# A two-layer diffusion trunk on one core: scheduling priority for the softmax steps, stores and bias tables placed anew, and four small changes of order

## The chip, the cores and the metric

One core of one Trainium2 chip runs the whole kernel in one launch. The metric is the device time of that launch in microseconds. TensorE (PE) does the matrix products and the transposes; VectorE (DVE), ScalarE (ACT) and GpSimd (POOL) do the elementwise work; SyncE (SP) issues most of the DMAs.

## The reference

The input is 1024 latent tokens and 256 context tokens of width 1024; there are two layers. Each layer is, per token group:

```python
h = rms_norm(x, norm_g) * (1 + scale) + shift          # shift, scale, gate from the conditioning
(aq, ak, av, ag, bq, bk, bv, bg, cx, cg, ga, gb, gc) = split(h @ w_in)
ya = window_attention(rope(norm(aq)), rope(norm(ak)), av, cached context k/v, sink) * silu(ag)
yb = neighbourhood_attention(rope(norm(bq)), ..., relative bias) * silu(bg)
yc = (linear_scan forward + backward of a gated recurrence on conv(cx)) * silu(cg)
z = sigmoid(ga) * (ya @ w_br[0]) + sigmoid(gb) * (yb @ w_br[1]) + sigmoid(gc) * (yc @ w_br[2])
x = x + gate * (z @ w_out)
```

Attention has 8 heads of 64 in each of two branches (A: a window of 128 tokens either side and a per-head sink; B: an 8 x 16 neighbourhood on the grid with a bias table). Latent queries read their local keys and 512 cached context keys in one softmax. All is float32; the kernel splits each operand in a high and a low part and does three products (or two) where it needs the precision.

## The kernel before, in words

Tokens lie along the free axis in three chunks: 0 and 1 are the latent halves of 512 tokens, 2 is the 256 context tokens. Activations have the 1024 features on 8 tiles of 128 partitions (`k`).

**Who sets the order.** PE's instructions run in the order in which the program emits them. A planner, `Weave`, sets that order: it has a clock of its own (`W.now`, in ns of estimated PE time), chains of dependent steps (the attention heads, the recurrence), and two queues of *dense* jobs (blocks of 24 matmuls of the input projection, `need` and `spare`) which it places where a chain is not yet due. `W.later(delay, fn)` runs `fn` when the clock has moved on by `delay`; `W.settle()` runs everything that is still waiting. The table `T` holds the delays. The dense blocks that stand between the steps of a chain are called filler below; they are finite in number. The other engines' order, and SP's, is made by a scheduler out of the whole program; `tc.high_priority(n)` lets what is emitted under it go ahead of other ready work that stands up to `n` places earlier, and `tc.keep_in_program_order` pins an instruction.

**Start (from `trunk`, `with pool("start")`).** The three chunks of x are loaded, transposed, normalised (`norm_apply`: on ACT `hhl`/`hhc`, on DVE `nt` and `hll`/`hlc`, for chunk 1 and chunk 2) while PE does gate blocks `gt`. `keep` stores the transposed x to DRAM (`x_d`), `constants` computes small per-layer columns, `bias_tables` builds B's bias tables through DRAM (`rp_d`, `t_d`, `bias_d`) with `W.later`. A gate block loads its weight (`wgt_r`, SP), casts it to the high part (`wgt_h`, ACT), subtracts for the low part (`wgt_l`, POOL), multiplies, and its result is copied (`tgt`, ACT) and stored (`g_d`, SP).

**Recurrence (`lru`).** Per feature block `f`, a conv on DVE (`xc`, split into `xh`, `xl`), then the gate products `lg`; `tiles["at", f]` is the planned time from which `lg` may be emitted.

**Attention (`attention`, `Group`).** Each branch has four pairs of heads (p = 0 to 3; B first, then A), each pair five groups of 256 queries (t0 = 0, 2, 8, 4, 6 in 128s; 8 is the context) with four score steps each. `score` (line 956) does: `sc`, the scores against the 512 cached keys (PE, one PSUM bank); DVE's minimum of `sc` (L976); `sl`, the local scores (PE, another bank); DVE's masked minimum (L992); for A the sink (L995 DVE, L996 ACT); ACT's two exponentials (L998 for `sc`, L1000 for `sl`). The banks `s` are two, so that the next `sc` has to wait for the exponential that frees its bank. `to_keys` transposes the exponentials (`pt`, three banks `t`) and splits them (`PT`, ACT L426 and DVE L427); `values` multiplies with V (`o`); `finish` adds and scales the result (Y: L1059 ACT, L1060 and L1066 DVE; `rt` is a transpose into a bank `t`). Beside it DVE and ACT normalise and rotate the next queries (`q_raw`, `q_sq`, `q_me`, L736 to L757).

**Merge and output.** `merge_jobs` makes `z`, `output_jobs` multiplies with `w_out` (blocks `po`, for chunks 0 and 2 together, then chunk 1), adds x, and in layer 0 takes the next layer's norm (`token_rstd`, whose product is `nps`, then `norm_apply`). A `tall` job goes through its features k once, for all of its chunks at each k; otherwise it finishes one chunk before the next.

## Time and profile before

| | |
|---|---|
| median of 3 runs | 3197.76 us (3196.37 to 3200.18) |
| the profiled execution | 3200.29 us, of which its span is 3198.5 us |
| PE busy | 3093.8 us (97%) |
| DVE busy | 1796.5 us (56%) |
| ACT busy | 1707.7 us (53%) |
| POOL busy | 974.9 us (30%) |
| granted PE clock, mean | 0.985 |
| moved by DMA | 435.03 MB, mean 136 GB/s |

PE is the engine that sets the time: the others are busy for little more than half of the span. As PE runs in the order of the program, any wait of one of its instructions holds up all that follow. A list of PE's waits gives, for each kind of waiting instruction, what released it, the total, how often and the longest; a timeline shows single instructions with the idle time before them and the releaser in square brackets. A table by windows gives PE's busy time and its granted clock (1.00 is full, 2.4 GHz; 0.50 is half, 1.2 GHz): busy time at half clock holds half the work.

### The profile page before, as it was taken

To read this page: it belongs to the slowest core of one execution; us is meant where nothing else is said; L and a number is where in the kernel's file an instruction comes from. 1 tells how busy PE (TensorE), PEld (TensorE's weight loads), DVE (VectorE), ACT (ScalarE), POOL (GpSimd) and SP (SyncE) were. 2 spreads that over 40 slices of the span, in tenths; PEclk is the share of its full clock that TensorE was granted. 3 is DMA by queue.
4 is the path that set the end of the run, shared out by engine and by line. 5 is a ranking of instruction groups with operands and counts; after the bars stand their busy time and mean duration, and the time that the engine had idled before them with its cause. 6 is when DMAs were issued, how large, how long until landed. Compare 5 with 4: busy or idle time off the path is not lost.

```text
span 3198.5 us, 48113 instructions
## 1 busy us (share of the span) xinstructions
PE 3093.8 (97%) x17421; PEld 2642.1 (83%) x17421; DVE 1796.5 (56%) x3293; ACT 1707.7 (53%) x3591; POOL 974.9 (30%) x815
## 2 busy tenths in 40 slices
PE   7899999999999999999999999999999999999999
PEld 5677788888888888888888778888888888888887
DVE  5565366666666664355464554665675666555531
ACT  5577355555555655443346864565555555544422
POOL 3554322223222121246343443221241222102632
PEclk9999999999999999999999999999999999999999
DMA  8554645535533232663442236545554333237543
GB/s 281 153 178 134 175 127 152 146 107 164 163 98 93 75 99 73 227 201 119 143 143 71 80 98 175 128 124 152 142 139 129 105 98 87 80 130 239 165 150 102
DMA packets 447434, 435.03 MB, mean 136 GB/s; under 512 B 75120, under 2 KB 368604, under 8 KB 445916
## 3 DMA queue, kind: packets, MB, share of 16 engines
q1 hardware_dynamic: 441212, 414.92, 43.6%
q0 software_dynamic: 5664, 16.83, 1.6%
q8 instruction: 137, 2.24, 0.3%
q14 instruction: 101, 0.83, 0.1%
q10 hardware_dynamic: 320, 0.21, 0.0%
HBM read 298.12 MB, written 137.29 MB: 136 GB/s over the span
## 4 chain that ended last, share of the span: by engine, by line
PE 78%; DVE 9%; ACT 4%; DMA 3%; issue 3%; POOL 2%; SPq 0%; ACTq 0%; DVEq 0%; POOLq 0%
PE gt L217 15%; PE sg L217 10%; PE br L217 7%; PE po L217 7%; PE o L217 6%; PE pt L224 6%; PE q L217 6%; PE k L217 4%; PE v L217 4%; PE sc L217 4%; PE sl L217 3%; PE cx L217 3%; PE lg L217 2%; DVE lR L686 1%; POOL acc L1236 1%
## 5 line engine op out<-in xcount | busy, mean ns | idle before, releaser
L426 ACT CAST PT<-pt 128x512 fp32r<-128x512 f32 (+2 forms) x528 | 272.5, 535 | 344.2 <-PE pt L224 340.0
L427 DVE TENSOR_TENSOR PT<-pt,PT 128x512 fp32r<-128x512 f32 (+2 forms) x528 | 321.9, 622 | 104.8 <-ACT PT L426 102.2
L976 DVE TENSOR_REDUCE st<-sc 128x1 f32<-128x512 f32 x256 | 176.6, 690 | 314.6 <-PE sc L217 314.2
L217 PE MATMUL gt<-hhl,wgt_h 128*128 128x512 f32 x736 | 301.5, 410 | 3.3 <-ACT wgt_h L421 3.3
L217 PE MATMUL gt<-hhl,wgt_l 128*128 128x512 f32 x736 | 292.5, 397 | 7.9 <-POOL wgt_l L422 7.9
L217 PE MATMUL gt<-hll,wgt_h 128*128 128x512 f32 x736 | 292.1, 397 | 0.0
L224 PE MATMUL pt<-cst,P 128*128 128x128 f32 x1856 | 271.8, 273 | 6.2 <-DVE Y L1066 3.8
L422 POOL TENSOR_TENSOR wgt_l<-wgt_r,wgt_h 128x512 fp32r<-128x512 f32 x110 | 176.6, 1613 | 324.4 <-ACT wgt_h L421 281.1
L224 PEld LDWEIGHTS pt<-cst,P 128*128 128x128 f32 x1856 | 217.2, 141 | 16.6 <-issue 7.8
L217 PE MATMUL po<-z,wpo_h 128*128 128x512 f32 (+1 forms) x768 | 212.9, 365 | 6.1 <-ACT z L426 4.9
L998 ACT ACTIVATE P<-sc,st 128x512 f32<-128x512 f32 x256 | 175.2, 684 | 57.9 <-DVE st L992 57.7
L217 PE MATMUL br<-yl,wbr_h 128*128 128x512 f32 (+1 forms) x576 | 205.1, 356 | 0.9 <-DVE yl L427 0.9
L217 PE MATMUL br<-yh,wbr_h 128*128 128x512 f32 (+1 forms) x576 | 204.7, 355 | 0.0
L217 PE MATMUL br<-yh,wbr_l 128*128 128x512 f32 (+1 forms) x576 | 204.4, 355 | 0.0
L217 PE MATMUL sc<-Kpast,Q 128*128 128x512 f32 x512 | 168.5, 410 | 28.6 <-ACT P L998 28.6
L422 POOL TENSOR_TENSOR wsg_l<-wsg_r,wsg_h 128x512 fp32r<-128x512 f32 x48 | 65.0, 1360 | 411.5 <-ACT wsg_h L421 289.2
L1000 ACT ACTIVATE P<-sl,st 128x384 f32<-128x384 f32 (+1 forms) x320 | 170.9, 534 | 16.0 <-DVE st L988 15.7
L217 PE MATMUL o<-PT,Vpast 128*128 128x256 f32 x1024 | 175.6, 292 | 3.6 <-DVE Y L1060 2.1
L217 PEld LDWEIGHTS gt<-hhl,wgt_l 128*128 128x128 f32 x736 | 139.9, 190 | 41.7 <-POOL wgt_l L422 9.2
L217 PEld LDWEIGHTS gt<-hhl,wgt_h 128*128 128x128 f32 x736 | 140.5, 191 | 34.8 <-issue 4.7
L217 PEld LDWEIGHTS po<-z,wpo_h 128*128 128x128 f32 x768 | 138.7, 194 | 29.5 <-ACT z L426 5.7
L217 PEld LDWEIGHTS gt<-hll,wgt_h 128*128 128x128 f32 x736 | 140.3, 191 | 25.5 <-issue 0.5
(350 smaller groups left out, 8562.7 us busy)
## 6 DMA issues: line engine op xcount, KB each, us to landing
Q<-q_d SPq DMA_DIRECT2D x160, 256.0 KB
gl<-g_d SPq DMA_DIRECT2D x48, 640.0 KB
wgt_r<-in_w_in_dram SPq DMA_DIRECT2D x110, 256.0 KB
g_d<-tgt SPq DMA_DIRECT2D x92, 256.0 KB
wa<-in_w_ada_dram POOLq DMA_DIRECT2D x64, 256.0 KB, 4.3
wpo_r<-in_w_out_dram SPq DMA_DIRECT2D x64, 256.0 KB
yg<-y_d SPq DMA_DIRECT2D x24, 640.0 KB
yr<-s_d SPq DMA_DIRECT2D x24, 640.0 KB
```

What stands on the lines that cost most here:

```text
L217: nc.tensor.matmul(out, a, b, start=start, stop=stop)
L224: nc.tensor.transpose(out, x, idn)
L422: nc.gpsimd.tensor_sub(lo, r, f32(hi))
L426: nc.scalar.copy(hi, x)
L427: nc.vector.tensor_sub(lo, x, f32(hi))
L686: nc.vector.tensor_tensor_scan(h, a, u, st if c0 < NLAT else 0.0, ALU.mult, ALU.add)
L976: nc.vector.tensor_reduce(cm, psc, AX.X, ALU.min)
L998: nc.scalar.activation(pt[:, nl * P:(nl + 4) * P], psc, AF.Exp, bias=m, scale=-1.0, accum_out=sums[:, t, x, 1:2])
L1000: nc.scalar.activation(pt[:, :nl * P], loc, AF.Exp, bias=m, scale=-1.0, accum_out=sums[:, t, x, 0:1])
L1236: (nc.vector if b == 0 and k >= KD - 2 else nc.gpsimd).tensor_add(z, z, g)
```

## The change

Seven edits:

- `score` runs under a priority of 400 (`AHEAD`), and so does the split of the transposed exponentials in `to_keys`.
- In layer 1, the gate products of the recurrence are planned 2500 ns later (`cv`), and the transposes of the cached keys (`kct`) 10000 ns behind their load where they were 7000 behind it.
- In layer 0's output, the norm's product for chunk 2 takes a bank `s` where it took the one bank `o`.
- The first block of `w_out` for chunks 0 and 2 is `tall`.
- At the start, the stores of x of chunks 1 and 2 come after both `norm_apply` and one by one, each behind one planned filler step; `constants` stands between the two chunks.
- Layer 1's rows of the bias tables are planned at 400000 + 20000 r ns where they were at 200000 + 3000 r.

```diff
--- before.py
+++ after.py
@@ -72,11 +72,12 @@
 
 
 EXP_LN = 6
+AHEAD = 400
 BEHIND = 2
 PSB = {"d": 2, "s": 2, "t": 3, "o": 1}
 LGB = ("s", "t")
 LDB = ("d", "t")
-T = dict(f1=9, f2=2, kc=7000, c0=10000, cq=1, gx=3, nx=8000, yo=1500, yi=1000, aq=9000, ac=7000, ms=2000, v=3200, tok=8600, scale=1100, t0=3400, tb=2200, o=2200, soft=7600, pace=9400, lg=320, lr=8500, cv=16000, le=4200)
+T = dict(f1=9, f2=2, kc=10000, c0=10000, cq=1, gx=3, nx=8000, yo=1500, yi=1000, aq=9000, ac=7000, ms=2000, v=3200, tok=8600, scale=1100, t0=3400, tb=2200, o=2200, soft=7600, pace=9400, lg=320, lr=8500, cv=16000, le=4200)
 
 
 class Weave:
@@ -621,7 +622,7 @@
             split(xh, xl, xc)
             W.mark(("conv", l, f))
             tiles[f] = (gh, gl, xc, xh, xl)
-            tiles["at", f] = W.now + T["cv"]
+            tiles["at", f] = W.now + T["cv"] + (2500 if l else 0)
 
         yield W.when(("cx", l, 0))
         conv(0)
@@ -954,6 +955,10 @@
 
 
             def score(g, s, i):
+                with tc.high_priority(AHEAD):
+                    g.score_of(s, i)
+
+            def score_of(g, s, i):
                 br, p = g.br, g.p
                 if g.st is None:
                     g.st = ap.tile([P, 36], F32, tag="st", name=f"st{g.name}", bufs=3)
@@ -1024,7 +1029,8 @@
                         transpose(pt[:, n * P:(n + 1) * P], g.P[g.units[s][i]][:, j * P:(j + 1) * P], ident)
                         n += 1
                 pq = ap.tile([P, 2, 512], F32R, tag="PT", name=f"PT{g.name}_{s}_{bi}", bufs=3)
-                split(pq[:, 0, :n * P], pq[:, 1, :n * P], pt[:, :n * P])
+                with tc.high_priority(AHEAD):
+                    split(pq[:, 0, :n * P], pq[:, 1, :n * P], pt[:, :n * P])
                 return pq
 
             def values(g, s, bank, pq, first, last):
@@ -1290,14 +1296,15 @@
                 add_square(l + 1, ci, k, xt, acc[ci], nc.vector.tensor_add)
 
                 def finish():
-                    token_rstd(l + 1, ci, acc[ci])
+                    token_rstd(l + 1, ci, acc[ci], "s" if ci == 2 else "o")
                     norm_apply(l + 1, ci, xs[ci], acc[ci], H)
                     W.mark(("x free", l, ci))
                 if k == KD - 1:
                     W.later(T["nx"], finish)
             return run
         return [(W.when(*[("Z", l, j) for j in range(KD)], *([("x free", l, free)] if free is not None and k else [])),
-                 job(I["w_out"][l], k * P, cis, lambda c: cols_of(Z, c), evac(k), f"po{l}_{cis[0]}_{k}"))
+                 job(I["w_out"][l], k * P, cis, lambda c: cols_of(Z, c), evac(k), f"po{l}_{cis[0]}_{k}",
+                     tall=len(cis) > 1 and k == 0))
                 for k in range(KD)]
 
 
@@ -1342,9 +1349,9 @@
             xs.append(xt)
         return xs
 
-    def keep(ci, xs):
+    def keep(ci, xs, ks=range(KD)):
         c0, N = CHUNKS[ci]
-        for k in range(KD):
+        for k in ks:
             ordered(dma(x_d[0][k][:, c0:c0 + N], xs[k][:, :N]))
 
 
@@ -1370,7 +1377,7 @@
                 W.later(20000 + 3000 * (3 * c + d), lambda c=c, d=d: shift(c, d))
         for l in range(DEPTH):
             for r in range(ROWS):
-                W.later(100000 + 100000 * l + 3000 * r, lambda l=l, r=r: rows(l, r))
+                W.later(400000 + 20000 * r if l else 100000 + 3000 * r, lambda l=l, r=r: rows(l, r))
 
     def fill(n):
         for _ in range(n):
@@ -1452,13 +1459,15 @@
             fill(T["f2"])
             token_rstd(0, 2, acc[2], "t", False)
             norm_apply(0, 1, xs[1], acc[1], H)
-            keep(1, xs[1])
             norm_apply(0, 2, xs[2], acc[2], H)
-            fill(9)
+            for ci in (1, 2):
+                for k in range(KD):
+                    fill(1)
+                    keep(ci, xs[ci], (k,))
+                fill(1)
+                if ci == 1:
+                    constants(0)
             starting.clear()
-            keep(2, xs[2])
-            constants(0)
-            fill(9)
             bias_tables()
         W.spare.extend((always, j((1, 2))) for j in jobs[:8])
         for l in range(DEPTH):
```

Three places in the order of the instructions show what the diff alone does not. Numbers behind a name are buffer numbers; the layer is left out of the names; lines of the changed kernel are a few higher.

**SP at the start, where the weight of gate block 7 (`wgt_0_70`) is loaded.** Before, right behind the stores of x of chunk 1:

```order
L1348 DMA x_d_6_78<-xi_6_719 128x512
L1348 DMA x_d_7_79<-xi_7_726 128x512
L413 DMA wgt_0_70_r_1082<-in_w_in_dram 128x4x128
L413 DMA wgt_0_70_r_1088<-in_w_in_dram 128x4x128
L413 DMA wcx_0_r_1134<-in_w_in_dram 128x4x128
L413 DMA wcx_0_r_1140<-in_w_in_dram 128x4x128
```

Now:

```order
L1355 DMA x_d_6_78<-xi_6_719 128x512
L711 DMA g_d_0_5_117<-tgt_0_50_0_1035 128x512
L1355 DMA x_d_7_79<-xi_7_726 128x512
L414 DMA wgt_0_70_r_1074<-in_w_in_dram 128x4x128
L414 DMA wgt_0_70_r_1080<-in_w_in_dram 128x4x128
L1355 DMA x_d_0_72<-xi_0_795 128x256
```

The loads now stand behind `g_d_0_5`, the store of the result of gate block 5, which reads the ACT copy `tgt_0_50`.

**ACT at the same place.** Before, the casts of that weight stood between the passes of `norm_apply` on chunk 1:

```order
L565 ACTIVATE hhl_2_234<-nt_1_2_935,mod_222 128x512
L565 ACTIVATE hhl_3_236<-nt_1_3_939,mod_222 128x512
L421 CAST wgt_0_70_0_h<-wgt_0_70_r_1082 128x512
L421 CAST wgt_0_70_4_h<-wgt_0_70_r_1088 128x512
L565 ACTIVATE hhl_4_238<-nt_1_4_943,mod_222 128x512
L565 ACTIVATE hhl_5_240<-nt_1_5_947,mod_222 128x512
```

Now they stand behind the passes on chunk 2 and two copies:

```order
L566 ACTIVATE hhc_4_985<-nt_2_4_983,mod_222 128x256
L566 ACTIVATE hhc_5_991<-nt_2_5_989,mod_222 128x256
L566 ACTIVATE hhc_6_997<-nt_2_6_995,mod_222 128x256
L710 COPY tgt_0_50_0_1035<-gt_0_50_0_914 128x512
L710 COPY tgt_0_60_0_1119<-gt_0_60_0_1086 128x512
L566 ACTIVATE hhc_7_1003<-nt_2_7_1001,mod_222 128x256
L422 CAST wgt_0_70_0_h<-wgt_0_70_r_1074 128x512
L422 CAST wgt_0_70_4_h<-wgt_0_70_r_1080 128x512
```

The copy `tgt_0_50` comes behind seven of the eight passes on chunk 2, and the casts behind all eight.

**DVE in branch A, p = 0, layer 0, from the first add of `Y_0_2` to the sink minimum of the first score step of group 4** (`st_0_4`). Before:

```order
L753 SCALAR_TENSOR_TENSOR q_1_1_raw<-q_1_1_sq,q_1_1_raw 128x512
L1060 TENSOR_TENSOR Y_0_2_9523<-o_0_2_9342,Y_0_2_9523 64x256
L757 STREAM_SHUFFLE q_1_1_sq<-q_1_1_raw 128x512
L1060 TENSOR_TENSOR Y_0_2_9523<-o_0_2_9342,Y_0_2_9523 64x256
L742 TENSOR_SCALAR q_1_2_me<-q_1_2_ms 128x256
L976 TENSOR_REDUCE st_0_4_9546<-sc_0_4_0_9548 128x1
L1066 TENSOR_TENSOR Y_0_2_9523<-Y_0_2_9523,rt_0_2_9560 128x256
L750 TENSOR_TENSOR q_1_2_raw<-q_1_2_raw,q_1_2_sq 128x256
L992 ISA sl_0_4_0_9552,st_0_4_9546<-sl_0_4_0_9552,mask_0_8743,st_0_4_9546 128x384
L992 ISA st_0_4_9546 128x1
L752 TENSOR_TENSOR q_1_2_sq<-q_1_2_me,q_1_2_sq 128x256
L995 TENSOR_TENSOR st_0_4_9546<-st_0_4_9546,sink_288 128x1
```

Now:

```order
L1066 TENSOR_TENSOR Y_0_2_9523<-o_0_2_9345,Y_0_2_9523 64x256
L754 SCALAR_TENSOR_TENSOR q_1_1_raw<-q_1_1_sq,q_1_1_raw 128x512
L1066 TENSOR_TENSOR Y_0_2_9523<-o_0_2_9345,Y_0_2_9523 64x256
L981 TENSOR_REDUCE st_0_4_9554<-sc_0_4_0_9556 128x1
L758 STREAM_SHUFFLE q_1_1_sq<-q_1_1_raw 128x512
L997 ISA sl_0_4_0_9560,st_0_4_9554<-sl_0_4_0_9560,mask_0_8746,st_0_4_9554 128x384
L997 ISA st_0_4_9554 128x1
L428 TENSOR_TENSOR PT_0_8_0_0_9573<-pt_0_8_0_0_9568,PT_0_8_0_0_9573 128x512
L1000 TENSOR_TENSOR st_0_4_9554<-st_0_4_9554,sink_288 128x1
```

Four passes of the query norm and the scaling of Y by `rt` went behind the sink minimum, the split of `PT_0_8` came in front of it, and the first add of Y now precedes the long pass `q_1_1_raw`.

**PE in the last group of layer 1's attention, around `sc_3_6_1`.** Before:

```order
L217 MATMUL sg_0_00_1_28559<-hhl_0_15404,wsg_0_00_0_l 128x512
L217 MATMUL sg_0_00_1_28559<-hhl_1_15406,wsg_0_00_0_h 128x512
L217 MATMUL sg_0_00_1_28559<-hll_1_15407,wsg_0_00_0_h 128x512
L217 MATMUL sg_0_00_1_28559<-hhl_1_15406,wsg_0_00_0_l 128x512
L217 MATMUL sc_3_6_1_28567<-Kpast_0_24169,Q_3_6_28327 128x512 x2
L217 MATMUL sl_3_6_1_28571<-Klat_0_24171,Q_3_6_28327 128x384 x2
L217 MATMUL o_3_4_28579<-PT_3_4_0_0_28539,Vpast_0_24453 128x256 x4
```

Now:

```order
L225 MATMUL pt_3_4_0_1_28607<-cst,P_3_4_0_28432 128x128
L225 MATMUL pt_3_4_0_1_28607<-cst,P_3_4_1_28472 128x128
L218 MATMUL sc_3_6_1_28616<-Kpast_0_24268,Q_3_6_28417 128x512 x2
L218 MATMUL sl_3_6_1_28620<-Klat_0_24270,Q_3_6_28417 128x384 x2
L218 MATMUL o_3_4_28628<-PT_3_4_0_0_28604,Vpast_0_24552 128x256 x4
L225 MATMUL pt_3_4_0_2_28633<-cst,P_3_4_0_28432 128x128
```

The filler (`sg_0_00`) is gone from in front of this score step, as from all places behind `sc_3_4_3`: 72 matmuls of it stood there before, and stand earlier now.

## Rows read from the trace of the kernel before

**Rows 1.** PE's waits: who waited, for whom; us in total, times, longest

```profile
PE sc L217 <- ACT P L998: 28.6, 12, 3.7
PE gt L217 <- POOL wgt_l L422: 7.9, 3, 5.9
PE lg L217 <- DVE xl L427: 5.5, 3, 1.8
PE pt L224 <- DVE Y L1066: 3.8, 2, 1.9
PE nps L217 <- DVE nw L533: 2.1, 1, 2.1
PE cx L217 <- ACT tgt L709: 1.8, 1, 1.8
PE kct L224 <- DMA kc<-in_cache_kb_dram: 1.8, 1, 1.8
```

**Rows 2.** PE's timeline, layer 0, branch A, p = 0: start us, us, instruction, [idle before]

```profile
918.69 0.39 PE L217 MATMUL gt<-hll,wgt_h 128*128 128x512 f32 x1
918.92 0.39 PE L217 MATMUL gt<-hhl,wgt_l 128*128 128x512 f32 x1
922.92 1.22 PE L217 MATMUL sc<-Kpast,Q 128*128 128x512 f32 x2 [3.61 <-ACT P L998]
```

**Rows 3.** DVE's timeline at the same place

```profile
914.43 1.66 DVE L753 SCALAR_TENSOR_TENSOR q_raw<-q_sq,q_raw 128x512 f32<-128x512 f32 x1
...
916.36 0.73 DVE L757 STREAM_SHUFFLE q_sq<-q_raw 128x512 f32<-128x512 f32 x1
...
917.91 0.68 DVE L976 TENSOR_REDUCE st<-sc 128x1 f32<-128x512 f32 x1
...
919.91 0.61 DVE L992 CUSTOM_DVE_ANT_0 sl<-sl,mask,st 128x384 f32<-128x384 f32 x1
...
921.31 0.56 DVE L995 TENSOR_TENSOR st<-st,sink 128x1 f32<-128x1 f32 x1
```

**Rows 4.** Windows: us; busy (count) of PE, PEld, DVE, ACT, POOL; granted clock; DMA share, GB/s

```profile
921.00:929.00 8.00, 6.08 (x18) 5.15 (x19) 4.22 (x9) 3.53 (x11) 3.19 (x5) 0.57 0.44 126
479.00:487.00 8.00, 6.35 (x29) 5.43 (x29) 6.03 (x13) 3.44 (x9) 3.64 (x5) 0.79 0.43 117
1595.00:1602.00 7.00, 5.93 (x19) 4.78 (x20) 6.52 (x9) 4.75 (x8) 1.67 (x1) 0.76 0.42 126
1759.00:1766.00 7.00, 5.17 (x24) 3.92 (x23) 5.05 (x7) 3.19 (x7) 3.67 (x2) 1.00 0.38 138
```

**Rows 5.** PE's timeline at the start, behind the wait for gate block 7's weight

```profile
95.50 0.79 PE L217 MATMUL gt<-hhl,wgt_l 128*128 128x512 f32 x1 [5.88 <-POOL wgt_l L422]
```

**Rows 6.** SP's timeline there: loads of weights

```profile
82.53 1.73 SPq L413 DMA_DIRECT2D wgt_r<-in_w_in_dram  x2
95.47 1.60 SPq L413 DMA_DIRECT2D wcx_r<-in_w_in_dram  x2
```

**Rows 7.** ACT's timeline there: the cast of a weight

```profile
98.37 0.62 ACT L421 CAST wcx_h<-wcx_r 128x512 fp32r<-128x512 f32 x1 [6.07 <-DMA wcx_r<-in_w_in_dram]
```

**Rows 8.** POOL's timeline there: low parts of weights, two in a row

```profile
79.72 2.79 POOL L422 TENSOR_TENSOR wgt_l<-wgt_r,wgt_h 128x512 fp32r<-128x512 f32 x2 [3.58 <-ACT wgt_h L421]
88.91 7.77 POOL L422 TENSOR_TENSOR wgt_l<-wgt_r,wgt_h 128x512 fp32r<-128x512 f32 x2 [6.41 <-ACT wgt_h L421]
```

**Rows 9.** DVE's timeline there: a pass of norm_apply

```profile
88.82 0.74 DVE L566 SCALAR_TENSOR_TENSOR hll<-nt,mod,hhl 128x512 fp32r<-128x512 f32 x1
```

**Rows 10.** PE's timeline, layer 1, last group: a score step

```profile
2832.15 0.62 PE L217 MATMUL sc<-Kpast,Q 128*128 128x512 f32 x2
```

**Rows 11.** ACT's timeline there: the exponential of that step

```profile
2835.15 0.67 ACT L998 ACTIVATE P<-sc,st 128x512 f32<-128x512 f32 x1
```

**Rows 12.** PE's timeline, layer 0, first block of w_out

```profile
1521.33 0.49 PE L217 MATMUL po<-z,wpo_h 128*128 128x512 f32 x1 [2.41 <-ACT z L426]
```

**Rows 13.** DVE's timeline there: the low part of the last z

```profile
1524.47 1.02 DVE L427 TENSOR_TENSOR z<-acc,z 128x512 fp32r<-128x512 f32 x2
```

## The prediction

> **What bounds the kernel now.** PE does, and it runs in program order, so I read its list of waits first [rows 1]; with the engines' busy times of the table it says that what can be gained is idle time of PE and the slow clock behind it, for no matmul is removed. One kind of wait is far ahead of the rest: `sc`, which waits for the exponential of L998, 28.6 us in 12 waits. The timeline showed that six of the twelve are alike, 3.5 to 3.7 us each, in the first score steps of group 4 of branch A at p = 0, 1 and 2 in both layers; one of them stands in [rows 2]: PE has finished its filler at 919.3 and starts `sc` at 922.92. Next I read the windows [rows 4]: busy time times (1 minus the granted clock) is what was lost to the half clock. Behind this wait it is 6.08 x 0.43 = 2.6 us. Behind the wait of 1.9 us for Y it is 6.35 x 0.21 = 1.3, behind that for the norm (2.1) 5.93 x 0.24 = 1.4, but behind the wait of 1.8 us of `lg` the clock is 1.00. So in these rows waits up to 1.8 cost themselves alone, and those from 1.9 on cost more than themselves. Last I followed each moved step on the other engines.
>
> **The change, part by part.** All sums are against the profiled execution, 3200.29 us, 2.5 above the median of the runs.
>
> *Priority of the score steps, the six long waits.* DVE's rows [rows 3] show why the exponential is late: the minimum of `sc` starts at 917.91 and the sink minimum, which releases ACT, at 921.31; between them stand foreign passes, and ahead of them the pass `q_raw` of 1.66 from 914.43. From the sink minimum to PE's restart it is 922.92 - 921.31 = 1.6 us. By the new order DVE does the first add of Y at 914.4, `q_raw` to 916.4, the second add to 916.8, the minimum (0.7) to 917.5, the shuffle (0.7) to 918.2, the masked minimum (0.6) to 918.8, the split (0.6) to 919.4, then the sink minimum; PE restarts at 919.4 + 1.6 = 921.0. PE itself arrives three matmuls later, which its order has in front of the first `sc` instead of behind it: 3 x 0.23 [rows 2], so at 920.0. The wait becomes 1.0 for 3.6, and by the rows above the clock then stays full. Six times 2.6 + 2.6 = **-31**. Bounds: 0 (the order helps nothing) and 6 x (3.6 + 2.6) = -37. The six shorter waits of the list, 28.6 - 6 x 3.65 = 6.7 in sum, hang on the same chain; I take half, **-3.5** (0 to -6.7).
>
> *What goes behind.* In branch B, p = 0, group 8, the scaling of Y (L1066) now stands behind a minimum, a masked minimum and a split, 0.6 to 0.7 each: 2.0 us later. There PE waits for it already, for a bank `t`: 3.8 in 2 waits, one per layer [rows 1]. Each grows by 2.0 and its slow clock by about 1: **+6** (0 to +10). In branch A the same delay meets no user of the bank before `sc`, so it costs nothing; without that cover each of the six would cost the same 2 to 3 us.
>
> *Norm in bank `s`.* The wait of `nps` goes, and its slow clock: 2.1 + 1.4 = **-3.5** [rows 1, 4].
>
> *`cv` in layer 1.* The three waits of `lg` go: **-5.5** (0 to -5.5). *`kc`*: the wait of `kct` goes: **-1.8** [rows 1].
>
> *The price of both.* They take filler early, and there is only so much. In the last group of layer 1's attention 72 matmuls of filler, 72 x 0.23 = 16 us, stood behind `sc_3_4_3`; now there are none. There a score step can't follow sooner than its predecessor's exponential ends: 2832.15 to 2835.15 + 0.67, 3.7 us [rows 10, 11]. PE's own work in a step is 1.5 to 2.6 us (an estimate: four wide products at 0.23 and 8 to 14 narrow ones at about half of it). Four steps leave 1 to 2.2 us idle each, 6 in all; the last transposes and products, where 18 of the filler matmuls stood, about 3 more; and as some of these waits reach 1.9, a slow clock at 1.3 to 1.4 each, three times, 4: **+13**. Lower bound 6 (the steps alone, full clock), upper bound the 16 of the filler and 6 of slow clock, 22.
>
> *The `tall` block.* PE now fills its wait for the last `z` (2.41 [rows 12]) with chunk 2's products. But the last `z` of chunk 2 is split by DVE only at 1524.47 + 1.02 = 1525.5 [rows 13], and DVE's order there is unchanged; PE is through with seven k's of both chunks by about 1521.5, so the wait moves from the middle of the block to its end. It ended at 1527.0 and ends at about 1526, with the slow clock now behind it: **+1** for both layers (-8 to +3).
>
> *Stores of x and constants at the start.* This is where I read SP's and ACT's order, for a late load. Gate block 7's weight was loaded at 82.53 [rows 6]; now the load stands behind the store of block 5's result, which waits for a copy on ACT that stands behind seven passes on chunk 2. DVE's pass at 88.82 [rows 9] is the eighth of sixteen on chunk 1; eight more at 0.66 end at 94.8, thirteen half ones at 0.4 (estimate) at 100, the copy at 101, and behind one more store the load is issued at 102. From issue to cast it is 98.37 - 95.47 = 2.9 [rows 6, 7], so the cast ends at 105.5. Then POOL makes the low part: either 7.77 for two, as it did here, or 2.79 for two, as at 79.72 [rows 8]. I take the second, 1.4 for the first half, since the passes of `norm_apply`, which ran through the first, are over by then. PE goes on at 106.9 instead of 95.5 [rows 5], +11.4. The wait for `tgt` (1.8, at 107) then finds its bank long free: **+9.6** (+5 to +14).
>
> The Trainium skill, "SBUF — State Buffer", section "Who interferes with whom", states that a DVE instruction with two SBUF inputs and a GpSimd instruction that reads SBUF exclude each other for the whole instruction. The two POOL rows differ by 2.8 times, and DVE's pass of [rows 9], with `nt` and `hhl` as inputs, lies within the slow one. By that rule the fast price holds from 102 on, as taken; by the slow row, the nearest in place, the first half would cost 3.9 instead of 1.4, and the sum would be 2.5 higher.
>
> *Bias rows of layer 1.* The recurrence of layer 0 ends with `W.settle()`, which runs everything that is planned, at whatever time; so the rows still stand in one batch in front of the first loads of layer 0's attention, eight where nine were. Nothing to speak of: **-0.5**. The two shorter waits of `gt` for a low part (7.9 - 5.9 [rows 1]) have their casts earlier in ACT's order now: **-2** (0 to -4).
>
> *Sum.* -31 - 3.5 + 6 - 3.5 - 5.5 - 1.8 + 13 + 1 + 9.6 - 0.5 - 2 = -18. From 3200.3 that is 3182, and 2.5 less for the median: **3180 us**.
>
> **The rivals.** *A, the banks and not the order hold up `sc`: slower.* There are two banks `s`, the change adds none, and if DVE's and ACT's new order only trades one late pass for another, the waits stay at 3.6. Then the -34.5 falls out: 3180 + 34.5 = 3214. For it: DVE is busy for nearly the whole stretch [rows 3], and the split that comes forward takes the place of what goes. Against it: the passes that go behind are longer in sum than what comes in front. It decides the sign once the six heads bring less than 11 of their 31. The Trainium skill, "Perfetto Trace Analysis", section "Optimization Strategy", says that the same gap repeating on the engine that should be saturated can mean too few buffers in PSUM or SBUF; six like gaps are such a pattern, and by that page this rival would hold.
>
> *B, the waits shrink but the clock still falls.* If the new wait is 2 and not 1 us, the slow clock of 2.6 stays at all six, and 1 us more of each wait: 3180 + 6 x 3.6 = 3202, slower too by the bound below, though hardly; half of the heads give 3191. For it: my chain leaves 0.8 us to the shortest wait that the clock punished.
>
> *C, the filler is not missed.* If the last group's steps, themselves now under priority, run in under 3 us, its +13 falls to 3, and the price at the start to 5: 3180 - 15 = 3165.
>
> *D, the price of the start or of the last group is double*: 3180 + 13 = 3193.
>
> **How the numbers follow.** Forecast (3172 to 3188) 0.45; C 0.20; B 0.13, of it 0.04 over 3204; D 0.10; A 0.12. A measurement of this kernel can tell about 0.2%, 6.4 us, from no change: faster is under 3191.4, slower over 3204.2. Faster takes the forecast, C, and part of B and D: 0.70. Same takes the rest of D and most of B: 0.14. Slower takes A and part of B: 0.16. The range reaches from C, with its smaller waits gone too, to B: 3156 to 3204; A is left out.
>
> **What would show it.** In the new profile: PE's list with `sc` at under 12 us and no `sc` wait over 2; windows behind them at clock 1.00; `pt` waiting for Y near 4 us, twice; `lg`, `nps` and `kct` gone; a wait of `gt` for a weight of some 18 us from 87 to 105; several waits of `sc` and `o` of 1 to 2 us in the last 35 us of layer 1's attention. The forecast is wrong if the `sc` waits stay over 3 us, or if the start shows no longer wait.

## The result, and the profile after

The changed kernel takes **3177.43 us** (median of 4 runs, 3174.76 to 3179.28) where the kernel before takes 3197.55 on the same chip: a ratio of 0.9935, 95% interval 0.9918 to 0.9953. That is 0.65% faster, by more than the 0.2% that a measurement can tell. The forecast was 3180 us, its range 3156 to 3204.

| | before | changed |
|---|---|---|
| span, us | 3198.5 | 3176.3 |
| PE busy, us | 3093.8 | 3081.1 |
| PE instructions | 17421 | 17421 |
| DVE, ACT, POOL busy, us | 1796.5, 1707.7, 974.9 | 1780.8, 1706.3, 969.8 |
| granted PE clock, mean | 0.985 | 0.989 |

PE does the same matmuls. Of the 22.2 us between the spans, 12.7 are busy time that PE no longer needs, because less of it runs at half clock, and 9.5 are idle time. From PE's list of waits in the changed kernel (who waited, for whom; us in total, times, longest):

```profile
PE gt L218 <- ACT wgt_h L422: 18.0, 1, 18.0
PE sc L218 <- ACT P L1003: 16.4, 15, 2.1
PE pt L225 <- DVE PT L428: 7.5, 8, 2.6
...
PE lg L218 <- DVE xl L428: 1.1, 1, 1.1
```

Against the list of the kernel before, of which [rows 1] shows a part: `sc` is down from 28.6 to 16.4, its longest wait from 3.7 to 2.1; `gt` has one wait of 18.0 in place of 7.9 in three for a low part and 3.3 in two for a high part (`wgt_h`); the waits of `lg` for `xl` are down from 5.5 to 1.1, the long one of `nps` for `nw` and that of `kct` are gone. The waits of `pt` for the split `PT` have grown from 1.2 in two, 0.6 at most, to 7.5 in eight, up to 2.6. The forecast's sign of `sc` under 12 and none over 2 did not come: 7.5 of the 16.4 stand in the last group of layer 1, outside of which `sc` waits 8.9 in all and 1.1 at most.

**The heads of branch A.** PE's timeline in layer 0, the first score step of group 4 at p = 0, 1 and 2:

```profile
920.08 0.74 PE L218 MATMUL sc<-Kpast,Q 128*128 128x512 f32 x2 [1.03 <-ACT P L1003]
1021.20 0.73 PE L218 MATMUL sc<-Kpast,Q 128*128 128x512 f32 x2 [1.02 <-ACT P L1003]
1122.36 0.73 PE L218 MATMUL sc<-Kpast,Q 128*128 128x512 f32 x2 [1.05 <-ACT P L1003]
```

3.61 became 1.03 [rows 2], and the pair of products takes 0.74 us instead of 1.22: the clock is full. The three of layer 1 wait 0.9, and in the 8 us behind each of the six the clock is 1.00. The windows around the first one (us; busy (count) of PE, PEld, DVE, ACT, POOL; clock; DMA share, GB/s) say the same, where [rows 4] had 0.57:

```profile
919.00:921.00 2.00, 0.97 (x5) 0.66 (x5) 1.54 (x5) 1.94 (x7) 1.92 (x3) 1.00 0.19 65
921.00:923.00 2.00, 2.00 (x13) 1.74 (x12) 1.82 (x3) 1.09 (x3) 1.86 (x3) 1.00 0.00 1
```

DVE's timeline at the same place answers to [rows 3]:

```profile
914.69 0.41 DVE L1066 TENSOR_TENSOR Y<-o,Y 64x256 f32<-64x256 f32 x1
915.03 0.67 DVE L754 SCALAR_TENSOR_TENSOR q_raw<-q_sq,q_raw 128x512 f32<-128x512 f32 x1
...
916.18 0.69 DVE L981 TENSOR_REDUCE st<-sc 128x1 f32<-128x512 f32 x1
...
917.54 0.61 DVE L997 CUSTOM_DVE_ANT_0 sl<-sl,mask,st 128x384 f32<-128x384 f32 x1
...
918.67 0.36 DVE L1000 TENSOR_TENSOR st<-st,sink 128x1 f32<-128x1 f32 x1
```

From the minimum to the sink minimum it is 2.5 us, where it was 3.4, and the minimum itself comes 1.7 us sooner, though the `sc` that it reads starts at the same time within 0.1 us (914.04 and 914.14). (The passes of the query norm that went behind the sink minimum are three, not four; with the scaling of Y they are four.) One part of that I had not counted: `q_raw` takes 0.67, not 1.66. POOL tells the likely reason. The pass `q_sq` just ahead of `q_raw` on DVE, and POOL's low part at that time, in the kernel before:

```profile
913.72 0.68 DVE L752 TENSOR_TENSOR q_sq<-q_me,q_sq 128x512 f32<-128x512 f32 x1
```

```profile
914.07 1.48 POOL L422 TENSOR_TENSOR wgt_l<-wgt_r,wgt_h 128x512 fp32r<-128x512 f32 x1 [1.80 <-ACT wgt_h L421]
```

And in the changed one:

```profile
913.50 1.27 DVE L753 TENSOR_TENSOR q_sq<-q_me,q_sq 128x512 f32<-128x512 f32 x1 [0.30 <-ACT q_sq L752]
```

```profile
912.93 1.28 POOL L423 TENSOR_TENSOR wgt_l<-wgt_r,wgt_h 128x512 fp32r<-128x512 f32 x1 [2.45 <-ACT wgt_h L422]
```

Before, the low part ran from 914.07 to 915.55, over the first 1.1 us of `q_raw` (914.43 to 916.09); now it is over at 914.21, before `q_raw` begins, but it runs over `q_sq` instead. So the cost of the overlap has moved more than it has gone: `q_raw` is 1.0 shorter, `q_sq` 0.6 longer, the two together 0.4 shorter. The Trainium skill, "SBUF — State Buffer", section "Who interferes with whom", states that a DVE instruction with two SBUF inputs and a GpSimd instruction that reads SBUF shut each other out, and these rows agree with it: whichever of the two passes the low part overlaps is the long one.

**The start.** Before, PE waited twice for gate block 7's weight, the second time the 5.88 us of [rows 5]; this is the first:

```profile
88.89 0.50 PE L217 MATMUL gt<-hhl,wgt_h 128*128 128x512 f32 x1 [1.91 <-ACT wgt_h L421]
```

Now, SP's load of that weight, ACT's cast, POOL's low part and PE, a fence for each engine:

```profile
100.38 0.32 SPq L711 DMA_DIRECT2D g_d<-tgt  x1
...
101.27 1.00 SPq L414 DMA_DIRECT2D wgt_r<-in_w_in_dram  x2
```

```profile
104.52 0.62 ACT L422 CAST wgt_h<-wgt_r 128x512 fp32r<-128x512 f32 x1 [3.27 <-DMA wgt_r<-in_w_in_dram]
```

```profile
105.22 2.50 POOL L423 TENSOR_TENSOR wgt_l<-wgt_r,wgt_h 128x512 fp32r<-128x512 f32 x2 [22.37 <-ACT wgt_h L422]
```

```profile
105.19 0.80 PE L218 MATMUL gt<-hhl,wgt_h 128*128 128x512 f32 x1 [18.02 <-ACT wgt_h L422]
...
106.54 0.79 PE L218 MATMUL gt<-hhl,wgt_l 128*128 128x512 f32 x1
```

The load is issued at 101.3 (82.53 before [rows 6]), behind the store that waits for ACT's copy, and PE stands from 87 to 105.2.

**The last group of layer 1.** PE's timeline of its score steps and, behind it, windows:

```profile
2795.01 0.85 PE L218 MATMUL sc<-Kpast,Q 128*128 128x512 f32 x2 [1.84 <-ACT P L1003]
2799.85 1.22 PE L218 MATMUL sc<-Kpast,Q 128*128 128x512 f32 x2 [1.99 <-ACT P L1003]
2805.01 1.22 PE L218 MATMUL sc<-Kpast,Q 128*128 128x512 f32 x2 [1.59 <-ACT P L1003]
2811.68 0.63 PE L218 MATMUL sc<-Kpast,Q 128*128 128x512 f32 x2
2815.49 0.85 PE L218 MATMUL sc<-Kpast,Q 128*128 128x512 f32 x2 [2.08 <-ACT P L1003]
```

```profile
2796.00:2802.00 6.00, 4.01 (x15) 3.32 (x15) 3.41 (x10) 2.67 (x8) 1.27 (x1) 0.50 0.33 100
2802.00:2808.00 6.00, 4.41 (x18) 3.81 (x17) 3.93 (x11) 2.60 (x7) 0.00 (x0) 0.50 0.01 3
2808.00:2814.00 6.00, 4.66 (x27) 3.73 (x25) 2.64 (x7) 3.21 (x9) 0.00 (x0) 0.91 0.00 0
2814.00:2820.00 6.00, 4.32 (x20) 3.96 (x20) 3.13 (x8) 2.99 (x11) 0.00 (x0) 0.72 0.00 0
```

No score step waited here before (one of them is [rows 10]); of these five, four wait 1.6 to 2.1 us, and behind them the clock falls to half for 12 us. Busy time times (1 minus clock) over these four windows is 2.0 + 2.2 + 0.4 + 1.2 = 5.8 us. The kernel before lost some of its own here, behind one wait of 2.1 us of `o` for Y, 0.5 + 0.8 = 1.3:

```profile
2842.00:2848.00 6.00, 3.75 (x25) 3.06 (x24) 4.35 (x8) 3.31 (x8) 1.67 (x2) 0.87 0.44 131
2848.00:2854.00 6.00, 4.92 (x27) 4.09 (x27) 1.98 (x3) 1.66 (x3) 0.00 (x0) 0.84 0.00 0
```

**A balance by stages.** Filler moves between stages, so start times alone don't compare. I took one named matmul at each border and subtracted from its start the usual full-clock time of every matmul that stands in front of it in that kernel's own order (the step from one to the next of its kind, out of both traces). What remains is PE time lost up to there, idle or at half clock. Its growth over a stage, less that of the kernel before, in us (B and A are the branches, e1 to e12 the runs below):

| stage | forecast | changed | e1 | e2 | e3 | e4 | e5 | e6 | e7 | e8 | e9 | e10 | e11 | e12 |
|---|---|---|---|---|---|---|---|---|---|---|---|---|---|---|
| start, to `cx` of chunk 1 | +9.6 | +9.6 | +2.4 | +0.1 | +9.7 | -0.1 | -1.0 | +8.0 | +9.6 | +8.9 | -1.0 | -0.6 | -0.7 | -0.7 |
| rest of layer 0 up to attention | -2.5 | -5.0 | -0.2 | +0.4 | -4.7 | -1.2 | -1.5 | -4.7 | -4.3 | -3.5 | +0.4 | 0.0 | +2.2 | +0.7 |
| B, layer 0 | +3 less part of 3.5 | -5.3 | -3.3 | -5.3 | -4.0 | -3.9 | -2.2 | -5.4 | -4.6 | -6.5 | -5.8 | -3.1 | -5.8 | -5.9 |
| A, layer 0 | -15.5 | -14.6 | -11.3 | -14.6 | -11.5 | -11.4 | -14.6 | -14.6 | -11.4 | -3.9 | -15.6 | +5.7 | -15.5 | -15.6 |
| merge, layer 0 | 0 | +2.5 | +2.9 | +2.7 | +1.4 | +0.7 | +2.7 | +2.8 | +5.6 | +1.6 | +0.9 | +2.0 | +1.1 | +1.5 |
| first `po` block | +0.5 | +1.9 | +0.2 | +0.5 | +1.8 | 0.0 | +1.2 | +0.4 | -0.8 | +0.7 | 0.0 | -1.0 | -0.1 | +1.8 |
| norm, chunk 2 | -3.5 | -4.0 | -1.6 | -4.0 | -4.0 | -4.0 | -4.0 | -4.0 | -4.0 | -4.0 | -4.0 | -4.0 | -4.0 | -4.0 |
| to the next gate block | 0 | +2.1 | +1.3 | +2.1 | +2.1 | +2.1 | +2.1 | +2.1 | +2.1 | +2.1 | +2.1 | +2.3 | +2.2 | +2.1 |
| recurrence, layer 1 | -5.5 | -6.8 | +2.4 | -7.0 | -0.2 | -0.8 | +0.8 | +2.0 | -7.0 | -7.0 | -0.8 | +1.9 | -7.1 | -7.2 |
| `kct`, layer 1 | -1.8 | -2.2 | -0.7 | -2.2 | -0.1 | -0.1 | -2.2 | -2.2 | -2.0 | -2.2 | -2.2 | -2.2 | -2.2 | -2.2 |
| B, layer 1 | +3 less part of 3.5 | -1.1 | -2.4 | -2.7 | -2.5 | -2.1 | +0.4 | +0.7 | -0.7 | -3.0 | -1.7 | -0.7 | -3.3 | -1.8 |
| A, layer 1 | -15.5 | -14.4 | -11.2 | -14.4 | -11.6 | -13.8 | -14.5 | -14.5 | -12.9 | -6.3 | -15.5 | +5.4 | -15.4 | -15.4 |
| last group, layer 1 | +13 | +16.6 | +1.0 | +16.5 | +0.6 | +0.1 | +1.7 | +1.7 | +12.7 | +13.0 | +0.6 | +3.1 | +0.6 | +0.6 |
| to the end | +0.5 | -1.1 | -1.0 | -0.8 | 0.0 | -0.7 | -1.9 | +0.2 | -1.4 | -0.4 | -1.5 | -1.5 | -1.8 | -1.1 |

The column of the changed kernel sums to -21.8, the difference of the spans being -22.2. These are single profiled executions, and a median can lie a few us away; another choice of the matmuls at the borders moves time between neighbouring cells, mostly 1 to 2 us, at places up to 5.

### The profile page after: what moved, and what is told of

It reads as the page before. It is cut to its first block, busy times and chain, and to the rows that moved or that the text cites. A ratio compares the mean times of both kernels' runs of the same rounds, so it can differ in the third digit from the quotient of the medians.

```text
span 3176.3 us, 48114 instructions
## 1 busy us (share of the span) xinstructions
PE 3081.1 (97%) x17421; PEld 2627.0 (83%) x17421; DVE 1780.8 (56%) x3293; ACT 1706.3 (54%) x3591; POOL 969.8 (31%) x815
## 4 chain that ended last, share of the span: by engine, by line
PE 78%; DVE 9%; ACT 5%; issue 3%; POOL 2%; DMA 2%; SPq 1%; ACTq 0%; DVEq 0%; POOLq 0%
PE gt L218 17%; PE sg L218 10%; PE o L218 7%; PE q L218 6%; PE pt L225 6%; PE po L218 5%; PE br L218 5%; PE k L218 4%; PE sc L218 4%; PE v L218 3%; PE cx L218 3%; PE sl L218 3%; POOL acc L1242 1%; PE lg L218 1%; DVE lR L687 1%
## 5 line engine op out<-in xcount | busy, mean ns | idle before, releaser
L218 PE MATMUL sc<-Kpast,Q 128*128 128x512 f32 x512 | 168.4, 410 | 17.0 <-ACT P L1003 16.4
```

Source lines behind the costliest of these rows:

```text
L218: nc.tensor.matmul(out, a, b, start=start, stop=stop)
```

## The experiments

**First set: the priority alone, and three parts put back.** e1 is the kernel before with the priority on `score` and on the split, and nothing else.

```diff
+                with tc.high_priority(AHEAD):
+                    g.score_of(s, i)
...
+                with tc.high_priority(AHEAD):
+                    split(pq[:, 0, :n * P], pq[:, 1, :n * P], pt[:, :n * P])
```

> The kernel before with the two priorities alone (score steps and the split of the transposed exponentials). My theory: the six waits of sc in group 4 of branch A go from 3.6 to 1.0 us and the half clock behind them goes, 27 to 28 us for the six, and branch B gains 5 to 7; the last group of layer 1 keeps its filler, so nothing is paid there: about 3163 us, 34 under the kernel before. Rival: the waits shrank in the changed kernel because its filler stands elsewhere (cv and kc), not for DVE's order; then this run keeps waits of over 3 us and stays above 3185.

3176.19 us, ratio 0.9932 [0.9919 to 0.9945]: the priority by itself gives as much as all seven edits together. It fell 13 us short of what I expected, in part because the pair p = 1 kept its wait, and its half clock (0.79 in the window from 1021 to 1029); PE's timeline of that head:

```profile
1022.23 1.14 PE L218 MATMUL sc<-Kpast,Q 128*128 128x512 f32 x2 [2.73 <-ACT P L1003]
```

The other two pairs wait 0.5, and 0.5 once more one step on. The waits of `lg` are about as long as before (1.85, 1.66 and 1.85 for three of 1.83), yet two of them are followed by a slow clock here (0.77 and 0.76 over the 7 us around them), and none was before (1.00).

e2 is the changed kernel with the stores of x and `constants` back in their old places.

```diff
-            for ci in (1, 2):
...
+            keep(1, xs[1])
...
+            fill(9)
+            starting.clear()
+            keep(2, xs[2])
+            constants(0)
+            fill(9)
```

> The changed kernel with the stores of x and the constants where they were before. My theory: the 18 us wait for gate block 7's weight comes from its load standing behind the store of block 5's result, so PE's idle time from 87 to 105 us falls back to about 8, and the run is 9.6 us faster than the changed kernel: about 3168 us. Rival: the load is late because the transfers of x use the DMA engines then, whatever the order; then the wait stays and the time too (3177).

3173.99 us, 0.9925 [0.9912 to 0.9937]. The long wait is gone (+0.1 in place of +9.6), but so is a gain of 5 us in the rest of layer 0's recurrence that came with it. By the balance the new order at the start costs about 4 net; the medians differ by 3.4, and the intervals of the two ratios overlap.

e3 is the changed kernel with `cv` and `kc` as before, both.

```diff
-T = dict(f1=9, f2=2, kc=10000, ...
+T = dict(f1=9, f2=2, kc=7000, ...
...
-            tiles["at", f] = W.now + T["cv"] + (2500 if l else 0)
+            tiles["at", f] = W.now + T["cv"]
```

> The changed kernel with cv and kc as before. My theory: the waits of lg and kct come back (6 to 8 us in the recurrence of layer 1), and the last group of layer 1's attention gets its 72 matmuls of filler back, worth 13 to 17 us: net 5 to 10 us faster than the changed kernel, 3167 to 3172 us. Rival: the last group loses its time to the priority (other work of DVE and ACT pushed behind the score steps) and not for want of filler; then the last group stays as slow and the run is 6 to 8 us slower than the changed kernel, about 3184.

3174.67 us, 0.993 [0.9917 to 0.9944], and the last group costs 0.6 in place of 16.6: its filler is back. The price of the two delays is thus shown. That they bring less than they cost is not: the medians differ by 2.8 us, and the intervals of the two ratios lie almost on one another. p = 1 has its wait of 2.7 again, as in e1; that this is `kc`'s doing, e5 and e7 show.

e4 is the kernel before with both priorities and the norm's product in a bank `s`.

```diff
-                    token_rstd(l + 1, ci, acc[ci])
+                    token_rstd(l + 1, ci, acc[ci], "s" if ci == 2 else "o")
```

> The kernel before with the two priorities and bank s for the norm's product of chunk 2, nothing else. My theory: 34 us from the priorities and 2 to 4 from the bank: 3159 to 3162 us, 15 us or more faster than the changed kernel. Rival: parts of the gain hang on the other edits (the tall block, the start), and the run is at 3170 or more.

3167.95 us, 0.9908 [0.9895 to 0.9922]. The norm brings -4.0 in every run that has it. It gives 2.1 of them back up to the next gate block, ahead of which PE now waits for the last weights of `w_out`, 0.67 and 0.62 us; the rest of the 2.1 was not traced. The run is 6 us above its forecast, as e1 was above its own.

**Second set: `cv` and `kc` apart, and the priority taken out.** e5 is e4 with `kc` at 10000.

```diff
-T = dict(f1=9, f2=2, kc=7000, ...
+T = dict(f1=9, f2=2, kc=10000, ...
```

> The kernel before with the two priorities, bank s for the norm's product and kc = 10000; cv, the w_out block, the start and the bias rows as before. By the stages of the first four runs kc is worth 2 to 3 us in branch B of layer 0, 3 us in the head p = 1 of branch A in each layer and 2 us at its own transposes, and it takes hardly any filler from the last group (66 matmuls stay there, by the order): about 3155 to 3159 us, 9 to 12 faster than priorities and bank alone (3168 there). Rival: what looked like the worth of kc in the changed kernel came from cv; then this run is within 3 us of 3168.

3163.96 us, 0.9897 [0.9883 to 0.9911]. All six heads now wait 0.9 to 1.1: p = 1 is down from 2.7, p = 0 and 2 are up from 0.5 (whose second wait is gone). As e5 differs from e4 in `kc` alone, this is its doing. By PE's order, the new `kc` makes the stretch ahead of all six heads alike: nine matmuls of filler where six stood, and 54 of q, k and v where there were 57, at p = 1 60. What the run misses of the expectation is mostly in B, 4.2 us worse than e4 by the balance, where `pt` waits for the split of P: 7.5 us in 8 waits, longest 2.6, as in the changed kernel.

e6 is the changed kernel with `cv` as before, e7 with `kc` as before.

```diff
-            tiles["at", f] = W.now + T["cv"] + (2500 if l else 0)
+            tiles["at", f] = W.now + T["cv"]
```

> The changed kernel with cv alone as before. Theory: cv alone takes the filler from layer 1's last group (by the order 66 matmuls stand there again, none with cv); the three waits of lg come back (6 us), the 17 us of the last group go: 11 us faster than the changed kernel, about 3166. Rival: the last group is slow for the priority's sake; then it stays slow and the run is 6 us slower, 3183.

```diff
-T = dict(f1=9, f2=2, kc=10000, ...
+T = dict(f1=9, f2=2, kc=7000, ...
```

> The changed kernel with kc alone as before. Theory: the head p = 1 of branch A keeps an sc wait of 2.7 us with slow clock in both layers (3 us each), branch B of layer 0 loses 2 to 3 us, kct waits again (2): about 10 us slower than the changed kernel, 3187. Rival: kc moves only the wait of kct; then 2 us slower, 3179.

e6 takes 3169.42 us (0.9911 [0.9898 to 0.9924]), e7 3180.07 (0.9939 [0.9926 to 0.9952]). Without the new `cv` the last group costs 1.7, without the new `kc` still 12.7: `cv` takes the last filler. It saves about 9 us of waits and slow clock in the recurrence (2.0 against -6.8) and costs 15 at the end; the medians differ by 8.0. e7 is only 2.6 us slower than the changed kernel, less than the runs can tell, where I expected 10: A did lose 3.2 and 1.5 with p = 1 back at 2.7, but the last group gave 3.9 back and `kct` did not wait again.

e8 is the changed kernel without either priority.

```diff
-                with tc.high_priority(AHEAD):
-                    g.score_of(s, i)
...
-                with tc.high_priority(AHEAD):
-                    split(pq[:, 0, :n * P], pq[:, 1, :n * P], pt[:, :n * P])
+                split(pq[:, 0, :n * P], pq[:, 1, :n * P], pt[:, :n * P])
```

> The changed kernel without the two priorities. Theory: the six sc waits of 3.6 us and the slow clock behind them come back (28 us), branch B loses some 5 us: about 33 us slower than the changed kernel, 3210, and 12 us slower than the kernel before. Rival: kc alone moves the order so that the six waits shrink without a priority; then under 3195.

3188.03 us, 0.9968 [0.9958 to 0.9978]. My expectation falls and the rival holds: the changed kernel loses 10.6 us without its priority, not 33. From its list of waits, and two of its heads in layer 0:

```profile
PE sc L217 <- ACT P L998: 26.3, 15, 2.7
```

```profile
921.50 0.73 PE L217 MATMUL sc<-Kpast,Q 128*128 128x512 f32 x2 [2.71 <-ACT P L998]
1025.98 1.22 PE L217 MATMUL sc<-Kpast,Q 128*128 128x512 f32 x2 [2.72 <-ACT P L998]
```

So the other edits alone bring the heads from 3.6 to 2.7, 10.2 us in both layers by the balance, and B gains 6.5 in layer 0 without any priority; which of the edits does that in B, no run shows by itself.

**Third set: the two priorities apart.** Both have the norm in a bank `s` and `kc` at 10000, and start, `cv` and `w_out` as before. e9 has the priority on `score` alone, e10 on the split alone.

```diff
+                with tc.high_priority(AHEAD):
+                    g.score_of(s, i)
```

> As the run with both priorities, bank s and kc = 10000 (3164 us), but the priority on the score steps alone, not on the split of the transposed exponentials. Theory: the six waits in branch A shrink because the score step's own passes on DVE move ahead of the query norm and of Y; by the order the sink minimum then has one pass of the norm in front of it (0.4 us) instead of the split (0.6): the waits stay at 1.0 us or fall to 0.8, and the products that wait for splits lose up to 3 us: 3160 to 3168 us. Rival: the split's priority carries the gain, by freeing the banks t early; then the run is 10 us or more slower, over 3174.

```diff
+                with tc.high_priority(AHEAD):
+                    split(pq[:, 0, :n * P], pq[:, 1, :n * P], pt[:, :n * P])
```

> The same with the priority on the split alone. Theory: DVE's order ahead of the sink minimum is as in the kernel before plus the split, so the six waits of sc stay at 2.6 us or more with the slow clock behind them: 15 to 20 us slower than with both (3164), about 3180 to 3184. Rival: the split's priority carries the gain; then within 4 us of 3164.

e9 takes **3156.64 us** (0.9871 [0.9855 to 0.9887]), 7 less than e5, which has the split's priority as well; by the balance 5.7 of it lie in B. e10 takes 3208.88 (1.0028 [1.0019 to 1.0037]), slower than the kernel before and 25 above what I expected. From their lists of waits, e9 first:

```profile
PE sc L218 <- ACT P L1003: 6.8, 12, 0.8
PE pt L225 <- DVE Y L1071: 6.0, 4, 2.4
```

```profile
PE sc L218 <- ACT P L999: 40.1, 35, 3.1
```

e10's 35 waits are not the six heads alone: in both layers the second score step of p = 1, 2 and 3 waits 1.6, where neither the kernel before nor any other run has a wait, as here at p = 1 of layer 0.

```profile
961.96 0.73 PE L218 MATMUL sc<-Kpast,Q 128*128 128x512 f32 x2 [1.61 <-ACT P L999]
```

DVE's timeline at the same head as above, of e10, shows the split in front of the masked minimum, which PE waits for:

```profile
914.29 0.68 DVE L977 TENSOR_REDUCE st<-sc 128x1 f32<-128x512 f32 x1
915.02 0.69 DVE L428 TENSOR_TENSOR PT<-pt,PT 128x512 fp32r<-128x512 f32 x1
...
915.96 0.62 DVE L993 CUSTOM_DVE_ANT_0 sl<-sl,mask,st 128x384 f32<-128x384 f32 x1
...
917.37 0.56 DVE L996 TENSOR_TENSOR st<-st,sink 128x1 f32<-128x1 f32 x1
```

And of e9, where it goes behind the sink minimum:

```profile
910.22 0.69 DVE L981 TENSOR_REDUCE st<-sc 128x1 f32<-128x512 f32 x1
...
911.57 0.61 DVE L997 CUSTOM_DVE_ANT_0 sl<-sl,mask,st 128x384 f32<-128x384 f32 x1
...
912.43 0.63 DVE L1000 TENSOR_TENSOR st<-st,sink 128x1 f32<-128x1 f32 x1
...
913.32 0.68 DVE L428 TENSOR_TENSOR PT<-pt,PT 128x512 fp32r<-128x512 f32 x1
```

With this the wait of the first head can be taken apart: how long before the end of PE's filler DVE starts the minimum, how long it is from there to the sink minimum, and from there to PE's restart (us, from the starts in the timelines; the end of the filler is PE's restart less its wait):

| | minimum ahead of PE | to the sink minimum | to PE | wait |
|---|---|---|---|---|
| before | 1.40 | 3.40 | 1.61 | 3.61 |
| e8, no priority | 1.87 | 2.97 | 1.61 | 2.71 |
| e10, split alone | 1.87 | 3.08 | 1.61 | 2.82 |
| changed | 2.87 | 2.49 | 1.41 | 1.03 |
| e9, score alone | 3.22 | 2.21 | 1.68 | 0.67 |

The edits other than the priority give 0.9, the score's priority some 2 more, the split's priority nothing at this head by itself, and beside the score's it takes 0.36 back. (e8 and e10 are compared across other edits too; the order of PE's filler around this head is the same in the last four rows.)

**Fourth set: the parts that pay, together.** e11 is e9 with `cv` put off by 1400 in place of 2500; by its order 66 matmuls of filler stay in the last group. e12 is e11 with the `tall` block.

```diff
-            tiles["at", f] = W.now + T["cv"]
+            tiles["at", f] = W.now + T["cv"] + (1400 if l else 0)
```

> Priority on the score steps alone, bank s, kc = 10000, and cv later by 1400 ns instead of 2500 in layer 1. By the order six filler matmuls more stand ahead of each late lg, and the last group keeps its 66; with 1800 or more it keeps none. Theory: the three waits of lg fall from 1.8 to 0.5 us and nothing is paid at the end: 4 us faster than without cv (3156.6), about 3152.5. Rival: the filler taken early is missed somewhere else in layer 1's attention: no gain, 3156 or more.

```diff
+                     tall=len(cis) > 1 and k == 0))
```

> The same with the tall first block of w_out. Theory: the wait for the last z only moves from the middle of the block to its end, and the next block's chunk 2 waits once more: 0 to 3 us slower than without it. Rival: the block hides its wait of 2.4 us in each layer and the slow clock behind: 4 us faster.

e11 takes **3151.25 us** (0.986 [0.9845 to 0.9875]), the best of all: 26 us under the changed kernel, 45 under the one before on its chip. The recurrence has all of `cv`'s gain (-7.1), and the last group costs 0.6. In it `lg` has no wait for `xl`, and `sc` waits 6.8 us in all, 0.8 at most, as in e9.

e12 takes 3152.88 (0.9865 [0.9848 to 0.9881]); 1.6 more is less than the runs can tell, but the balance has the block itself at +1.8 against -0.1.

## Why the prediction was right, and where it was not

The total, the direction and the large places came out as forecast; two of the terms had the wrong cause or sign. That the sum fits as well as it does is in part luck: B came out 8.9 us better than its terms, while A, the merge, the first `po` block, the next gate block and the last group together came out 11.6 worse.

*The six long waits: -31 forecast, -29.0 by the balance.* The wait of 1.0 and the full clock behind it are there, and the working of the wait holds: forecast 3.2 from the minimum's start to the end of PE's filler, 2.6 to the sink minimum, 1.6 to PE's restart; measured 2.87, 2.49 and 1.41. The step that failed is the cause: I booked the whole 31 under the priority, though three matmuls of the working are filler that no priority moves. The priority alone gives 22.5 (e1), the rest of the change alone 10.2 (e8). `kc` moves that filler in front of these steps, and with the old `kc` one pair in three keeps 2.7 us (e1, e3, e4, e7). The two gains don't add up to 29.0. And of the two priorities the score's does the work; the split's, which I had let pass as one that "takes the place of what goes", costs 7 us beside the other and makes e10 11 us slower than the kernel before (3208.88 against 3197.81), although e10 has the norm's bank and `kc` too.

*Y behind, +6: the sign failed.* In B, group 8 of p = 0, the bank `t` was to come free 2 us later, behind the scaling of Y. In the changed kernel PE waits there for the split, which DVE starts 0.6 us ahead of that scaling, since the split has priority too:

```profile
486.35 0.66 PE L225 MATMUL pt<-cst,P 128*128 128x128 f32 x4 [2.63 <-DVE PT L428]
```

The wait grew by 0.7, not 2.0 (in e9, without the split's priority, PE does wait for Y there, 2.4 at most, so 0.5 more), and layer 0 has no slow clock behind it, where [rows 4] had 0.79; layer 1 has it still. B as a whole won 5.3 and 1.1 where my terms (+6 and -3.5) had it lose 2.5. That is not the priority's doing alone: e8 has 6.5 without it, e1 3.3 without the rest.

*The start, +9.6: measured +9.6.* The load was issued at 101.3 for 102 forecast, the cast ended at 105.1 for 105.5. I priced POOL's low part at 2.79 for two rather than 7.77; it took 2.50, with DVE idle, as the rule in the Trainium skill's "SBUF — State Buffer", section "Who interferes with whom", would have it. PE's first two products need the high part alone and start from 105.2 on; the first that needs the low part, the one of [rows 5], starts at 106.5 for 106.9. The term that was missing is behind it: the rest of layer 0's recurrence gives back 5.0, not 2.5. Two waits there that I had not looked at are gone or shorter: 1.4 of `gt` for a high part, and that of `lg` for `mod`, 2.0 with a clock of 0.91 around it (170 to 190), which is 0.9 with the clock at 1.00 (190 to 210). Against them, `lg` now waits 1.1 for `xl` and 1.5 for `lJ` (0.7 before), and `adat` 1.0. e2 shows that the gain belongs to the start's order; which of its moves makes it was not tried.

*The last group, +13: 16.6, within the bounds.* Its listed waits are 12.0 us where there were 3.2, so 8.8 more, for 9 forecast; the slow clock lost 5.8 in the four windows above where it had lost 1.3, so 4.5 more, for 4. The other 3 are in neither list: they are lost between matmuls that the trace counts as busy, and their cause stays open. That the filler and not the priority makes the price, e8 shows: without a priority its four steps wait the same 1.84, 1.99, 1.59 and 2.08.

*Small terms.* The six shorter waits of `sc`, -3.5: 7.0 us in all before, 3.1 now. Norm -3.5: -4.0, but 2.1 are given back. `cv` -5.5: -6.8. `kct` -1.8: -2.2. The two short waits for a low part, -2: gone from the list of the changed kernel, and 1.4 of them are back with the old start (7.3 less 5.9 in e2). The bias rows of layer 1 had no run of their own; what lost 2.5 in the merge of layer 0 was not traced. The `tall` block +1: +1.9 in layer 0, and the wait did move to chunk 2's last product, which answers to [rows 12]:

```profile
1512.37 1.08 PE L218 MATMUL po<-z,wpo_h 128*128 128x256 f32 x2 [2.25 <-ACT z L427]
```

*The rivals.* A, that the banks and not the order hold up `sc`, is refuted: e9 has the same two banks `s` and waits of 0.8 at most. The page of the Trainium skill that spoke for it ("Perfetto Trace Analysis", section "Optimization Strategy": a repeating gap can mean too few buffers) says "can", and here it does not. B failed too, since no head kept its slow clock. C fell with the 16.6 of the last group, D with its size. Two figures in the weighing of the rivals are off, without weight in the end: with 18 us of gain forecast, A turns the sign once the heads bring less than 13, not 11, of their 31, and from 1.0 to the shortest wait with a slow clock, 1.9, it is 0.9, not 0.8.

## What to carry to other kernels

A wait for a buffer that repeats may come from where the releasing step stands in another engine's queue: split it into how early the chain starts, how long it is and how soon the waiter arrives, before buffers are added. Give priority to the chain that the engine that sets the time waits for, and try each further priority in the same queue by itself: here the second cost 7 us beside the first. Independent matmuls that fill waits are a finite stock, so each delay that draws them forward must be priced where the last of them stood; a smaller delay (1400 for 2500) kept both gains.

## What the runs showed of the hardware that I had not expected

How long a wait is does not by itself tell whether the clock falls behind it. I had read from [rows 4] that waits up to 1.8 us cost themselves alone and those from 1.9 on more. Windows of 8 us, which hold most of a wait of 2.7 or 2.8 us in this same place and the 5 to 7 us behind it, say otherwise, e8 (p = 0 and p = 1 of layer 0) first, then e10 (p = 1):

```profile
919.00:927.00 8.00, 5.50 (x19) 4.42 (x20) 4.60 (x10) 3.53 (x12) 3.77 (x5) 0.79 0.45 131
1024.00:1032.00 8.00, 6.02 (x17) 5.06 (x18) 4.08 (x8) 3.53 (x11) 3.25 (x5) 0.58 0.46 135
```

```profile
1026.00:1034.00 8.00, 6.62 (x33) 5.52 (x34) 3.85 (x8) 3.52 (x11) 2.71 (x4) 1.00 0.52 147
```

With 2.71 us the mean granted clock was 0.79, with 2.72 it was 0.58, with 2.83 it was full. In the 8 us of filler ahead of each of them PE was busy throughout, at clock 1.00 (for instance 1016 to 1024 in e10). Nor are the shorter ones alike: around the waits of 1.85 us of `lg` in e1 it was 0.77 and 0.76, around those of 1.83 in the same place before 1.00. In the changed kernel the 2.6 us in B are followed by a full clock in layer 0 and 0.79 in layer 1 (2040 to 2048):

```profile
482.00:490.00 8.00, 5.37 (x29) 4.42 (x28) 6.50 (x15) 4.80 (x12) 3.15 (x3) 1.00 0.29 78
2040.00:2048.00 8.00, 5.41 (x22) 4.35 (x21) 6.46 (x14) 4.68 (x12) 3.15 (x3) 0.79 0.49 103
```

What decides it, these runs leave open. A forecast does better to price such a wait with the slow clock as a chance than as a fixed price.
